# Gate and up weights of 32 experts: two strided transfers of 512 KB per tile, or one of 1 MB from weights laid out as tiles

## The chip, the cores and the metric

The kernel runs on one core of one Trainium2 chip. The metric is the device time of one execution in microseconds; the median of a few runs counts. One further execution was taken by the hardware profiler, and every row below comes from it.

## The reference, cut to what matters

One transformer block over 512 tokens of width 2048 in float32: a mixer (retention and a state space model), a mixture of 32 experts with two experts per token, a gated side input, and a last norm. The change touches only the weights of the experts:

```python
def expert_block(args):              # toks: the tokens of one block of expert e
    e, toks = args
    xb = ht[toks]
    a = jax.nn.silu(xb @ w_gate[e]) * (xb @ w_up[e])     # 2048 x 512 each
    return a @ w_down[e]                                 # 512 x 2048
```

Each expert has 4 MB of gate, 4 MB of up and 4 MB of down weights, 384 MB in all, and all of them are read.

## The kernel before

Three stages follow one another. The mixer takes the first 1300 us or so. Then comes the loop over the experts, in pairs (`pr`, two experts `ee` each), to about 2430 us. The last stage is the gated side input with its own weights.

**Tiles and their ring.** Every weight of an expert is loaded into SBUF as a tile of 128 partitions x 8 KB (1 MB). An expert takes 12 such tiles: 8 for gate and up (`load_gu`, q = 0 to 7) and 4 for down (`load_expert`). `mtile` hands out the tiles in turn from a ring of 13: six of pool `mwx` (on the right side of SBUF) and seven of pool `mw`. A transfer into a tile waits until TensorE has read what the tile held 13 tiles earlier. After expert 28 `mwx` is given up for other buffers (`right = False`), and experts 29 to 31 have a ring of seven.

**What a gate and up tile holds.** Partition p of tile q holds rows q*256 + p and q*256 + 128 + p of the gate and of the up matrix, in the order (k, w, f): k is the half of the 256 rows, w is gate or up, f the 512 columns. In HBM, gate and up are two tensors with rows of 512 floats, 2 KB. So a tile takes two transfers of 512 KB, one for gate and one for up, and each moves runs of 2 KB: two per partition. A down tile is 128 whole rows of 2048 floats: one transfer of 1 MB in runs of 8 KB.

**Order of the work.** All these transfers are issued by SyncE (SP), one after the other, in the order of the loop. TensorE (PE) also works in order. For one expert it runs 64 matmuls over the 8 gate and up tiles (line 991, into `pg`), waits for the activation on ACT and DVE (lines 994 to 996), transposes it (999), and runs 32 matmuls over the 4 down tiles (1008, into `py`). For a pair it also gathers the tokens (`dispatch_ids`, an indirect transfer of 1 MB issued by POOL into `xo`, line 854), transposes them (877), and adds the results into the residual (`combine`, 32 matmuls of line 1031 with additions on DVE, mixed with the next expert's gate and up matmuls). The matmul of one half k of a tile reads gate and up of that half together, so it needs both transfers of the tile.

**Beginning and end.** The first six tiles of expert 0 are loaded during the last product of the mixer; the others when that product's buffers are given up. The routing of the tokens to experts must be done before the first matmul of expert 0. In expert 29 `ple_side` loads the side input and its weights between q = 3 and q = 4, and its matmuls (1073) are mixed into the work of experts 29 to 31.

Behind the loop stands a second use of `load_expert`, for tokens beyond 64 of one expert; it is a loop over a count that is known only at run time.

Of the kernel before, what the change touches and what calls it, by code (L numbers as in the profile page):

```python
# [29 lines left out]
E, F = 32, 512  # L30
# [11 lines left out]
def kernel(ctx, tc, A, out):  # L42
    nc = tc.nc
# [93 lines left out]
    hT, wu = [], []  # L137
# [218 lines left out]
    for b in range(NB):  # L356
# [22 lines left out]
        for i, src in enumerate((c_re, c_im)):  # L379
            for g in range(2):  # L380
                q = slice(g * 64, (g + 1) * 64)
# [302 lines left out]
    ss2 = x1pool.tile([128, 4, 4], FT, name="ss2", bufs=1)  # L684
    lg = x1pool.tile([128, 512], FT, name="lg", bufs=1)

    wg_a, wu_a, wd_a = A["w_exp_gate"], A["w_exp_up"], A["w_exp_down"]
    NX, NM = 6, 7
    n_mw = 0
    right = True  # L690
# [1 line left out]
    def mtile():  # L692

        nonlocal n_mw
        n = n_mw % (NX + NM)
        n_mw += 1
        if right and n < NX:
            return mwx.tile([128, 2048], FT, name="mwx", tag="mwx", bufs=NX)
        return mw.tile([128, 2048], FT, name="mw", tag="mw", bufs=NM)

    def load_gu(wg, wu, q):
        t = mtile().rearrange("p (k w f) -> p k w f", k=2, w=2)
        for n, w in enumerate((wg, wu)):
            nc.sync.dma_start(t[:, :, n, :], w[q * 256:(q + 1) * 256, :].rearrange("(k p) f -> p k f", p=128))
        return t

    def load_expert(wg, wu, wd, between=None, have=()):
        gu, dn = list(have), []
        for q in range(len(gu), 8):
            if q == 4 and between is not None:  # L710
                between()
            gu.append(load_gu(wg, wu, q))
        for q in range(4):
            t = mtile()
            nc.sync.dma_start(t, wd[q * 128:(q + 1) * 128, :])
            dn.append(t)
        return gu, dn

    first = []
    for cb in range(4):  # L720
        sl = slice(cb * 512, (cb + 1) * 512)

        def ev_o(i, p, cb=cb, sl=sl):
            xn = x2[i][:, sl]
            V.tensor_tensor(xn, p, xn, op=OP.add)
            S.dma_start(x1_d[i * 128:(i + 1) * 128, sl], xn)
            jk = opool.tile([128, 512], FT, name="jk", tag="xt")
            S.activation(jk, xn, AF.Square, accum_out=ss2[:, i, cb:cb + 1])
        dense(A["w_out"], D, cb * 512, mT, "tok", ev_o)
        while len(first) < min(NX, 2 * (cb + 1)):  # L730
            first.append(load_gu(wg_a[0], wu_a[0], len(first)))
        pl = ps("pl")
        for d in range(4):
            pt = ps("pt")
            for i in range(4):
                PE.transpose(pt[:, i * 128:(i + 1) * 128], x2[i][:, cb * 512 + d * 128:cb * 512 + (d + 1) * 128], ident)
            xt = opool.tile([128, 512], FT, name="xt", tag="xt")
            (S.activation(xt, pt, AF.Copy) if d % 2 else V.tensor_copy(xt, pt))
            o = (d % 2) * 64
            PE.matmul(pl[o:o + 64, :], wr[:, cb * 4 + d, :], xt, start=d < 2, stop=d >= 2)  # L740
        if cb == 0:
            V.tensor_copy(lg, pl)
        else:
            V.tensor_tensor(lg, pl, lg, op=OP.add)
# [15 lines left out]

    io512 = mo.tile([128, T], FT, name="io512", bufs=1)
    with tc.high_priority(offset=8000):
        first = load_expert(wg_a[0], wu_a[0], wd_a[0], have=first)
    nc.sync.dma_start(io512, A["c_iota"])
    rtmp = tc.alloc_tile_pool(name="rtmp", bufs=1, reuse_waits="tile")

# [312 lines left out]
    for pr in range(E // 2):  # L1079
        _, xo, xg, tk1, _ = disp  # L1080
        nxt, sw_n = disp, sw
        ys = ytiles()
        for e in range(2):
            ee = pr * 2 + e
            if ee == E - 1:
                wg0 = gate_w(0, 0, 0, mtile().rearrange("p (k c) -> p k c", k=4))
            wts = load_expert(wg_a[ee], wu_a[ee], wd_a[ee], ple_side if ee == E - 3 else None) if ee else first
            if e == 0 and pr + 1 < E // 2:
                nxt = dispatch_ids(pr + 1)
                sw_n = dispatch_scales(nxt[0], pr + 1)  # L1090

            def xcol(kt):
                if ee == 0 and kt % 4 == 0:
                    dispatch_part(xo, xg, kt // 4)
                if kt % 2 == 0 and (ee != E - 3 or kt >= 8):
                    next(side, None)
                return xg[:, kt, e * CAP:(e + 1) * CAP]
            expert(wts, xcol, sw[:, e, 1:2], sw[:, e, 0:1], ys, e)
            if e == 0 and pr + 1 < E // 2:
                for d4 in range(4):  # L1100
                    dispatch_part(nxt[1], nxt[2], d4)
            if ee == E - 4:
                right = False
                mwx.release()
                x1pool.release()
                ple = tc.alloc_tile_pool(name="ple", bufs=1, side="right", reuse_waits="tile")
        disp = nxt
        sw = sw_n
        if pr == E // 2 - 1:
            for _ in side:  # L1110
                pass
        combine(ys, [tk1[:, v:v + 1] for v in range(2)])
# [5 lines left out]
    with tc.For_i(0, nov, 1) as bi:  # L1118
        ereg = nc.values_load(ctl_d[0:1, bass.ds(bi, 1)], engines=[mybir.EngineType.SP], min_val=0, max_val=E - 1,
                              skip_runtime_bounds_check_because="an expert's number, at most E - 1")  # L1120
        tbo = mo.tile([128, 4], FT, name="tbo", bufs=1)
        for hf in range(2):
            nc.sync.dma_start(tbo[hf * 64:hf * 64 + CAP], tbl_d[bass.ds(bi * CAP + E * CAP, CAP), :])
        oi = mo.tile([128, 1], I32, name="oi", bufs=2)
        V.tensor_scalar(oi, tbo[:, 0:1], 0.0, None, op0=OP.max)
        tko = mo.tile([128, 2], FT, name="tko", bufs=1)
        V.memset(tko, 0.0)
        for g in range(2):
            V.tensor_scalar(tko[g * 64:(g + 1) * 64, g:g + 1], tbo[g * 64:(g + 1) * 64, 0:1], 1.0, None, op0=OP.add)
        xo = xtile([128, D], "xo", "xo")  # L1130
        GP.indirect_dma_start(out=xo, out_offset=None, in_=x1_d,
                              in_offset=bass.IndirectOffsetOnAxis(ap=oi[:, 0:1], axis=0))
        xgo = xtile([128, 16, 128], "xgo")
        for d in range(16):
            px = ps("px")
            PE.transpose(px[:, :128], xo[:, d * 128:(d + 1) * 128], ident)
            V.tensor_scalar(xgo[:, d], px[:, :128], nffn[:, d:d + 1], None, op0=OP.mult)
        wts = load_expert(*(w[bass.ds(ereg, 1)].rearrange("o a b -> (o a) b") for w in (wg_a, wu_a, wd_a)))
        ys = ytiles()
        for y_ in ys:  # L1140
            V.memset(y_.bitcast(FT), 0.0)
        expert(wts, lambda kt: xgo[:, kt, 0:64], tbo[:, 1:2], tbo[:, 2:3], ys, 0)
        combine(ys, [tko[:, v:v + 1] for v in range(2)])
# [107 lines left out]
def host_arrays(inp):  # L1251

    g = {}
    f = np.ascontiguousarray
    g["x"] = f(inp["x"][0])
    g["xT"] = f(inp["x"][0].T)
    for k in ("norm_mix", "norm_ffn", "norm_ple"):
        g[k] = f(inp[k][0].reshape(16, 128).T)
    for k in ("w_in", "w_merge", "w_glu", "w_branch_a", "w_branch_b", "w_out",
              "w_exp_gate", "w_exp_up", "w_exp_down", "w_ple_gate", "w_ple"):  # L1260
        g[k] = f(inp[k][0])

    qk = g["w_in"][:, :2 * W].reshape(D, H, 2, 2, DH // 2).transpose(0, 1, 3, 2, 4).reshape(D, 2 * W)
    g["w_in"] = np.concatenate([qk, g["w_in"][:, 2 * W:]], axis=1)

    def gp(a):
        return a[0].reshape(NJ, 2, P, -1).transpose(1, 2, 0, 3).reshape(128, -1)

    ldt = np.broadcast_to(inp["ssm_log_dt"][0].reshape(NJ, 2).T[:, None, :], (2, P, NJ)).reshape(128, NJ)
    cr, ci = (inp[k][0].transpose(0, 2, 1)[None] for k in ("ssm_c_re", "ssm_c_im"))  # L1270
    dd = np.broadcast_to(inp["ssm_d"][0].reshape(NJ, 1, 2, C).transpose(1, 2, 3, 0), (L, 2, C, NJ)).reshape(128, NJ)
    g["s5_par"] = np.concatenate(
        [gp(inp["ssm_lam_re"][..., None]), gp(inp["ssm_lam_im"][..., None]), ldt, gp(inp["ssm_b_re"]),
         gp(inp["ssm_b_im"]), gp(cr), gp(ci), dd], axis=1)
    g["ret_gn_w"] = f(inp["ret_gn_w"][0].reshape(H, DH).T)
    g["norm_f"] = f(inp["norm_f"])
    g["pT"] = f(inp["p"][0, 0].T)
    g["w_router"] = f(np.concatenate([inp["w_router_group"][0], inp["w_router_expert"][0]], axis=1)
                      .reshape(16, 128, 36).transpose(1, 0, 2))
    g["b_router"] = np.concatenate([inp["b_router_group"][0], inp["b_router_expert"][0]])  # L1280
    return g
# [62 lines left out]
```

## Time and profile before

| what | us |
|---|---|
| median of 3 runs | 2632.17 (2630.09 to 2633.79) |
| the profiled execution, its own time | 2631.76 |
| its span, first to last instruction | 2630.0 |
| PE busy | 2470.2 (94%) |
| DVE busy | 1128.9 (43%) |
| ACT busy | 569.8 (22%) |
| mean granted TensorE clock | 0.987 of full |

The span is the stretch that the profile's rows cover; the profiled execution took 1.76 us more than its span. Ends of matmuls are modelled, and a matmul counts as busy also where it passes slowly, so PE at 94% is not PE at its peak. Two further things about the rows: times to landing of a transfer count from its issue, so they hold the time that it queues behind others; and the share of the DMA engines can come out somewhat over 1, since packets overlap.

### The profile page before, as it was taken

The numbers are of one execution on the slowest core, as the hardware profiler recorded it, in microseconds if no ns is written. First come the engines' busy times: TensorE is split into PE (matmuls) and PEld (weight loads), VectorE is DVE, ScalarE is ACT, GpSimd is POOL, SyncE is SP. The second block draws the span as 40 slices with busy tenths as digits, with TensorE's granted clock in tenths as the row PEclk, the third lists the DMA queues.
The fourth block names the chain that finished last, engine by engine and source line by source line (L and its number), as shares of the span: only waits on it lengthen the run. The fifth ranks groups of instructions, "written<-read, shape, count | busy, mean of one in ns | idle before, by whom it ended". The sixth has DMA issues, their size and how long they took to land. (4 is left out here: it accounts for less than half of the span.)

```text
span 2630.0 us, 28248 instructions
## 1 busy us (share of the span) xinstructions
PE 2470.2 (94%) x11178; PEld 1590.9 (60%) x11178; DVE 1128.9 (43%) x2204; ACT 569.8 (22%) x722; POOL 134.0 (5%) x166
## 2 busy tenths in 40 slices
PE   8999999999999999999969998888888888888998
PEld 7888788888888888887733333333333333323886
DVE  6648965333423443532244333333333333323535
ACT  4243222231221232222211000000000000012534
POOL 1010000002102010000010000000000000000101
PEclk9999999999999999999989999999999999999999
DMA  8332333442222245562279999999999999986333
GB/s 298 104 105 93 112 110 115 158 156 96 97 96 96 89 158 181 195 224 96 80 263 398 398 398 398 398 398 398 398 398 398 398 398 398 399 319 219 127 109 128
DMA packets 266023, 618.07 MB, mean 235 GB/s; under 512 B 19986, under 2 KB 28690, under 8 KB 246050
## 3 DMA queue, kind: packets, MB, share of 16 engines
q1 hardware_dynamic: 260208, 593.04, 61.9%
q0 software_dynamic: 3376, 19.01, 1.8%
q10 hardware_dynamic: 2306, 4.20, 0.4%
q8 instruction: 90, 1.47, 0.2%
q14 instruction: 43, 0.35, 0.0%
HBM read 591.01 MB, written 25.23 MB: 234 GB/s over the span
## 5 line engine op out<-in xcount | busy, mean ns | idle before, releaser
L63 DVE TENSOR_TENSOR wl<-wst,wh 128x2048 fp32r<-128x2048 f32 (+1 forms) x111 | 251.5, 2266 | 412.0 <-ACT wh L62 411.9
L103 PE MATMUL acc<-hTh,wh 128*128 128x512 f32 x832 | 327.9, 394 | 11.7 <-ACT wh L62 6.8
L62 ACT ACTIVATE wh<-wst 128x2048 fp32r<-128x2048 f32 (+1 forms) x111 | 207.5, 1869 | 605.6 <-PE acc L104 353.5
L104 PE MATMUL acc<-hTl,wh 128*128 128x512 f32 x832 | 328.5, 395 | 0.0
L105 PE MATMUL acc<-hTh,wl 128*128 128x512 f32 x832 | 326.0, 393 | 0.1
L991 PE MATMUL pg<-mw,xg 128*64 128x512 f32 x1136 | 289.6, 599 | 19.1 <-DMA mw<-in_w_exp_up_dram 19.1
L991 PE MATMUL pg<-mwx,xg 128*64 128x512 f32 x912 | 230.6, 600 | 10.0 <-DMA mwx<-in_w_exp_up_dram 9.4
L991 PEld LDWEIGHTS pg<-mw,xg 128*64 128x64 f32 x1136 | 81.2, 136 | 181.2 <-issue 177.4
L103 PEld LDWEIGHTS acc<-hTh,wh 128*128 128x128 f32 x832 | 157.4, 189 | 46.5 <-ACT wh L62 6.8
L1032 DVE TENSOR_TENSOR x<-pc,x 128x512 f32<-128x512 f32 x256 | 161.6, 684 | 40.8 <-PE pc L1031 40.4
L995 DVE SCALAR_TENSOR_TENSOR sg<-pg,sw,sg 128x256 f32<-128x256 f32 x32 | 15.5, 483 | 378.7 <-ACT sg L994 378.7
L104 PEld LDWEIGHTS acc<-hTl,wh 128*128 128x128 f32 x832 | 157.4, 189 | 33.2 <-issue 0.8
L105 PEld LDWEIGHTS acc<-hTh,wl 128*128 128x128 f32 x832 | 157.4, 189 | 33.2 <-DVE wl L63 0.8
L1016 DVE SCALAR_TENSOR_TENSOR ysl<-py,sw,ysh 64x512 fp32r<-64x512 f32 x128 | 94.8, 750 | 188.2 <-ACT ysh L1015 183.6
L1008 PE MATMUL py<-mw,aT 128*64 128x512 f32 x640 | 154.5, 622 | 4.1 <-DVE aT L1001 4.1
L1015 ACT ACTIVATE ysh<-py,sw 64x512 fp32r<-64x512 f32 x128 | 87.2, 682 | 293.8 <-PE py L1008 289.0
L991 PEld LDWEIGHTS pg<-mwx,xg 128*64 128x64 f32 x912 | 66.8, 137 | 136.3 <-issue 134.8
L994 ACT ACTIVATE sg<-pg,sw 128x256 f32<-128x256 f32 x32 | 15.2, 474 | 577.7 <-PE pg L991 577.7
L1031 PE MATMUL pc<-ysh,oht 128*128 128x512 f32 x256 | 107.5, 429 | 22.7 <-ACT ysh L1015 22.4
L1031 PEld LDWEIGHTS pc<-ysh,oht 128*128 128x128 f32 x256 | 48.5, 190 | 93.4 <-DVE x L1032 48.8
L1031 PE MATMUL pc<-ysl,oht 128*128 128x512 f32 x256 | 100.9, 404 | 0.0
L105 PE MATMUL acc<-wh,hTl 128*128 128x512 f32 x256 | 100.8, 394 | 0.0
(354 smaller groups left out, 3615.6 us busy)
## 6 DMA issues: line engine op xcount, KB each, us to landing
mw<-in_w_exp_down_dram SPq DMA_DIRECT2D x80, 1024.0 KB, 14.7
mw<-in_w_exp_gate_dram SPq DMA_DIRECT2D x142, 512.0 KB, 10.9
mw<-in_w_exp_up_dram SPq DMA_DIRECT2D x142, 512.0 KB, 10.8
mwx<-in_w_exp_gate_dram SPq DMA_DIRECT2D x114, 512.0 KB, 10.8
mwx<-in_w_exp_up_dram SPq DMA_DIRECT2D x114, 512.0 KB, 10.8
mwx<-in_w_exp_down_dram SPq DMA_DIRECT2D x48, 1024.0 KB, 15.8
wst<-in_w_in_dram SPq DMA_DIRECT2D x39, 1024.0 KB, 5.0
wst<-in_w_merge_dram SPq DMA_DIRECT2D x32, 1024.0 KB, 5.9
```

Of the source, the lines that this page charges most:

```text
L62: S.activation(hi, src, AF.Copy)
L63: V.tensor_sub(lo, src, hi.bitcast(FT))
L103: PE.matmul(acc, s0, m0, start=first, stop=False)
L104: PE.matmul(acc, s0, m1, start=False, stop=False)
L105: PE.matmul(acc, s1, m0, start=False, stop=last)
L991: PE.matmul(pg[hf * 64:(hf + 1) * 64, :], xk, gu[kt // 2][:, kt % 2, :, hf * 256:(hf + 1) * 256], start=kt == 0, stop=kt == 15)
L995: V.scalar_tensor_tensor(sg, pg[:, 0:256], rcol, sg, op0=OP.mult, op1=OP.mult)
L1008: PE.matmul(pys[c2][ch * 64:(ch + 1) * 64, :], aT[:, kc % 2, (kc // 2) * 64:(kc // 2 + 1) * 64], dn[kc][:, c0:c0 + 512], start=kc == 0, st ...
L1015: S.activation(yh[q, c0:c0 + 512], pys[c2][q], AF.Copy, scale=wcol[q])
L1016: V.scalar_tensor_tensor(yl[q, c0:c0 + 512], pys[c2][q], wcol[q], yh[q, c0:c0 + 512].bitcast(FT), op0=OP.mult, op1=OP.subtract)
L1031: PE.matmul(pc, oh[cb // 2][:, i * 128:(i + 1) * 128], ys[n][:, sl], start=n == 0, stop=n == 1)
L1032: V.tensor_tensor(x2[i][:, sl], pc, x2[i][:, sl], op=OP.add)
```

## The change

On the host, gate and up of each expert are written into one array in the order of the tiles: (expert, q, partition, k, w, f). Row q*128 + p of the new array is what partition p of tile q holds, 2048 floats, 8 KB in one piece. The kernel then loads a tile with one transfer of 1 MB. What lies where in SBUF is the same, and so is every matmul. The rest of the diff passes the one tensor where two were passed.

```diff
-    wg_a, wu_a, wd_a = A["w_exp_gate"], A["w_exp_up"], A["w_exp_down"]
+    wgu_a, wd_a = A["w_exp_gu"], A["w_exp_down"]
...
-    def load_gu(wg, wu, q):
-        t = mtile().rearrange("p (k w f) -> p k w f", k=2, w=2)
-        for n, w in enumerate((wg, wu)):
-            nc.sync.dma_start(t[:, :, n, :], w[q * 256:(q + 1) * 256, :].rearrange("(k p) f -> p k f", p=128))
-        return t
-
-    def load_expert(wg, wu, wd, between=None, have=()):
+    def load_gu(wgu, q):
+        t = mtile()
+        nc.sync.dma_start(t, wgu[q * 128:(q + 1) * 128, :])
+        return t.rearrange("p (k w f) -> p k w f", k=2, w=2)
+
+    def load_expert(wgu, wd, between=None, have=()):
...
-            gu.append(load_gu(wg, wu, q))
+            gu.append(load_gu(wgu, q))
...
-            wts = load_expert(wg_a[ee], wu_a[ee], wd_a[ee], ple_side if ee == E - 3 else None) if ee else first
+            wts = load_expert(wgu_a[ee], wd_a[ee], ple_side if ee == E - 3 else None) if ee else first
...
+    gu = np.empty((E, 8, 128, 2, 2, F), np.float32)
+    for n, k in enumerate(("w_exp_gate", "w_exp_up")):
+        gu[:, :, :, :, n] = inp[k][0].reshape(E, 8, 2, 128, F).transpose(0, 1, 3, 2, 4)
+    g["w_exp_gu"] = gu.reshape(E, 8 * 128, 4 * F)
```

## Rows read from the trace of the kernel before

**Rows 1.** The page: 40 slices of 65.75 us; DMA busy tenths, GB/s, packets.

```profile
DMA  8332333442222245562279999999999999986333
GB/s 298 104 105 93 112 110 115 158 156 96 97 96 96 89 158 181 195 224 96 80 263 398 398 398 398 398 398 398 398 398 398 398 398 398 399 319 219 127 109 128
DMA packets 266023, 618.07 MB, mean 235 GB/s; under 512 B 19986, under 2 KB 28690, under 8 KB 246050
```

**Rows 2.** The page, DMA issues: count, size, median us from issue to landing.

```profile
mw<-in_w_exp_down_dram SPq DMA_DIRECT2D x80, 1024.0 KB, 14.7
mw<-in_w_exp_gate_dram SPq DMA_DIRECT2D x142, 512.0 KB, 10.9
...
mwx<-in_w_exp_gate_dram SPq DMA_DIRECT2D x114, 512.0 KB, 10.8
```

**Rows 3.** Windows: length, busy of PE, PEld, DVE, ACT, POOL; clock, DMA share, GB/s.

```profile
1496.00:1512.00 16.00, 16.00 (x79) 5.76 (x81) 5.52 (x8) 2.73 (x4) 0.00 (x0) 1.00 1.05 386
1526.00:1542.00 16.00, 14.51 (x59) 6.77 (x55) 10.50 (x17) 2.73 (x4) 0.00 (x0) 1.00 1.05 387
1516.00:1522.00 6.00, 3.74 (x18) 1.05 (x16) 1.39 (x3) 0.47 (x1) 0.00 (x0) 1.00 1.01 421
1550.00:1558.00 8.00, 7.33 (x34) 2.16 (x30) 0.12 (x1) 0.47 (x1) 0.00 (x0) 1.00 1.02 423
...
1483.94:2274.88 790.94, 701.59 (x3122) 261.48 (x3120) 284.69 (x503) 76.90 (x120) 14.10 (x12) 0.98 1.04 398
```

**Rows 4.** Timeline of PE, one expert: start, us, line, [idle before <- releaser].

```profile
1699.43 7.04 PE L991 MATMUL pg<-mwx,xg 128*64 128x512 f32 x32
1707.12 1.94 PE L991 MATMUL pg<-mw,xg 128*64 128x512 f32 x8 [0.66 <-DMA mw<-in_w_exp_up_dram]
...
1715.23 1.94 PE L991 MATMUL pg<-mw,xg 128*64 128x512 f32 x8 [0.76 <-DMA mw<-in_w_exp_up_dram]
```

**Rows 5.** Timeline of POOL: the gathers of the tokens, one for each pair.

```profile
1483.94 1.18 POOL L854 DMA_INDIRECT xo<-x_d,oi  x1 [59.31 <-DVE oi L852]
...
1746.25 1.16 POOL L854 DMA_INDIRECT xo<-x_d,oi  x1 [66.36 <-DVE oi L852]
...
2274.88 1.17 POOL L854 DMA_INDIRECT xo<-x_d,oi  x1 [66.11 <-DVE oi L852]
```

**Rows 6.** Timeline of PE, from expert 0 to expert 2.

```profile
1374.59 0.41 PE L999 MATMUL pt<-ident,sg 128*128 128x128 f32 x2 [1.70 <-DVE sg L996]
...
1385.65 10.47 PE L991 MATMUL pg<-mwx,xg 128*64 128x512 f32 x48
...
1407.38 1.88 PE L991 MATMUL pg<-mw,xg 128*64 128x512 f32 x6
...
1433.28 0.44 PE L999 MATMUL pt<-ident,sg 128*128 128x128 f32 x2 [1.60 <-DVE sg L996]
```

**Rows 7.** Timeline of SP: issues at the beginning of the experts.

```profile
1335.91 0.47 SPq L704 DMA_DIRECT2D mw<-in_w_exp_up_dram  x1
1359.32 0.37 SPq L704 DMA_DIRECT2D mwx<-in_w_exp_gate_dram  x1
```

**Rows 8.** Waits of SP from 1484 to 2275: us, times, longest.

```profile
SPq L704 <- PE pg L991: 54.0, 22, 6.5
```

**Rows 9.** Timeline of PE: expert 29's last gate and up tile.

```profile
2315.78 1.94 PE L991 MATMUL pg<-mw,xg 128*64 128x512 f32 x8 [0.77 <-DMA mw<-in_w_exp_up_dram]
2319.41 0.41 PE L999 MATMUL pt<-ident,sg 128*128 128x128 f32 x2 [1.70 <-DVE sg L996]
```

**Rows 10.** Windows, as in rows 3: the first six tiles' loading, and experts 29 to 31.

```profile
1140.00:1180.00 40.00, 40.00 (x180) 33.13 (x179) 10.67 (x10) 8.37 (x10) 0.00 (x0) 1.00 0.81 280
2319.00:2430.00 111.00, 102.19 (x350) 35.55 (x350) 35.89 (x58) 19.72 (x32) 0.00 (x0) 0.98 0.69 251
```

**Rows 11.** DMA issues from 1483.94 to 2274.88: the gathers, median us to landing.

```profile
xo<-x_d,oi POOLq DMA_INDIRECT x12, 11.3
```

**Rows 12.** Timeline of PE: the first transposes of gathered tokens after 1746.

```profile
1757.78 0.77 PE L877 MATMUL px<-ident,xo 128*128 128x128 f32 x5
```

More of the change, by code (lines that the diff above doesn't have):

```diff
@@ L730 @@
         while len(first) < min(NX, 2 * (cb + 1)):
-            first.append(load_gu(wg_a[0], wu_a[0], len(first)))
+            first.append(load_gu(wgu_a[0], len(first)))
         pl = ps("pl")
@@ L762 @@
     with tc.high_priority(offset=8000):
-        first = load_expert(wg_a[0], wu_a[0], wd_a[0], have=first)
+        first = load_expert(wgu_a[0], wd_a[0], have=first)
     nc.sync.dma_start(io512, A["c_iota"])
@@ L1137 @@
             V.tensor_scalar(xgo[:, d], px[:, :128], nffn[:, d:d + 1], None, op0=OP.mult)
-        wts = load_expert(*(w[bass.ds(ereg, 1)].rearrange("o a b -> (o a) b") for w in (wg_a, wu_a, wd_a)))
+        wts = load_expert(*(w[bass.ds(ereg, 1)].rearrange("o a b -> (o a) b") for w in (wgu_a, wd_a)))
         ys = ytiles()
@@ L1259, in host_arrays @@
     for k in ("w_in", "w_merge", "w_glu", "w_branch_a", "w_branch_b", "w_out",
-              "w_exp_gate", "w_exp_up", "w_exp_down", "w_ple_gate", "w_ple"):
+              "w_exp_down", "w_ple_gate", "w_ple"):
         g[k] = f(inp[k][0])
+    gu = np.empty((E, 8, 128, 2, 2, F), np.float32)
+    for n, k in enumerate(("w_exp_gate", "w_exp_up")):
+        gu[:, :, :, :, n] = inp[k][0].reshape(E, 8, 2, 128, F).transpose(0, 1, 3, 2, 4)
+    g["w_exp_gu"] = gu.reshape(E, 8 * 128, 4 * F)
     qk = g["w_in"][:, :2 * W].reshape(D, H, 2, 2, DH // 2).transpose(0, 1, 3, 2, 4).reshape(D, 2 * W)
```

## The prediction

> **What bounds the kernel now.** I read the page's 40 slices first. The mixer and the last stage move 80 to 225 GB/s in most slices; in 14 slices, from about 1380 to 2300 us, the DMA engines are busy all the time and the rate stands at 398 GB/s without moving [rows 1]. A rate that doesn't move while the work on the other engines changes is the sign of a stage bound by transfers. The DMA issues say what is moved there: 256 gate tiles and as many up tiles of 512 KB (two names each, 142 and 114), and 128 down tiles of 1 MB [rows 2].
>
> Next I looked into the stage in short windows, to see whether 398 is one rate or a mean of two. It is a mean. While gate and up tiles pass, the engines move 386 or 387 GB/s; while down tiles (or the gather of the tokens) pass, 421 or 423, with the DMA share at 1.0 in both [rows 3]. The reader is to see that the two kinds differ in the length of their runs (2 KB and 8 KB), and that no engine's work goes along with it: in 1496 to 1512 PE is always busy and in 1526 to 1542 nearly so, at the same rate.
>
> Then I asked whether PE feels it. In the timeline of PE its matmuls over gate and up stand in groups of 8, one tile each, and at the end of an expert each group begins with a wait for a transfer: four groups begin from 1707.12 to 1715.23, 8.11/3 = 2.70 us apart [rows 4]. A tile of 1,048,576 bytes at 386.5 GB/s takes 2.713 us. So PE gets its tiles at the pace at which gate and up come in. Over many pairs: the gathers of the tokens begin 790.94/12 = 65.91 us apart [rows 5], and 12 is the number of pairs between the first and the last of them. In 65.91 us the queue moves 16 gate and up tiles, 8 down tiles and 1 MB of tokens. Taking 16 x 2.713 = 43.4 off, 22.5 us are left for 9 MB in 8 KB runs, 2.50 us each (419 GB/s). The windows and the pairs agree.
>
> **What PE would do without this wait.** At the beginning 13 tiles lie ready: the last of them is issued at 1335.91, and the next waits until 1359.32, when TensorE has freed one [rows 7]. So the first pairs show PE on its own. From the transpose in expert 0 (1374.59) to the same in expert 2 (1433.28) it takes 58.69 us, with 48 matmuls in 10.47 us in one piece and no transfer named before it [rows 6]. That is the other bound: a pair can't go under some 58.7 us, and 65.91 leaves 7.2 us of it as waiting.
>
> **The change part by part.**
>
> *The runs.* Each gate and up tile becomes what a down tile is now: 128 runs of 8 KB, 1 MB in one piece of HBM, one transfer, the same place in SBUF. The nearest row for its cost is thus the down tile itself. Bounds: 2.479 us (423 GB/s) and 2.506 us (22.55/9, the gather included). I take 2.50, since it comes from whole pairs and not from picked windows. A tile saves 2.713 - 2.50 = 0.213 us.
>
> *How many tiles count.* All that pass while the queue never runs dry. That begins with tile 13 (expert 1, q = 1) at 1359.32 and ends with expert 29, whose last tile PE still waits for at 2315.78 [rows 7, 9]. Expert 1 has 7 such tiles, experts 2 to 28 have 27 x 8 = 216, expert 29 has 8: 231. So 231 x 0.213 = 49.2 us. Expected pair: 16 x 2.50 + 9 x 2.50 = 62.5 us, 3.4 less than now and 3.8 above PE's 58.7; PE stays the one that waits.
>
> *Tiles that don't count.* The first six of expert 0 are loaded at 1140 to 1165 beside a PE that is busy 40 of 40 us [rows 10]; the next seven lie ready before the routing ends. Worth nothing, and if they were late they would cost no more than their own shortening. In experts 29 to 31 after 2319 the DMA share is 0.69 and PE is busy 102 of 111 us [rows 10]: PE sets the pace, and 16 faster tiles give 0 to 3.4 us. I take 0.
>
> *The issues.* 256 transfers fewer are issued by SP, 0.4 us each [rows 7]. SP is ahead of the transfers by the 10.8 us to landing [rows 2], so this is worth nothing now. If that cover were gone, 231 x 0.4 us would lie between transfers; fewer issues can only help then.
>
> *The waits.* A matmul needed gate and up of a tile, so it waited for the later of two; now it waits for one. Nothing becomes coarser. The ring stays at 13 tiles. SP waits for a free tile 54 us in 12 pairs, at most 6.5 us at once [rows 8], and the engines' share doesn't fall meanwhile [rows 3], since 10.8 us of transfers are queued. A faster queue runs ahead by some 38 us (the rest of a pair after a starved stretch, about 15 tiles) x 5% = 0.7 tile more, so the queue falls by about 2 us and still covers 6.5.
>
> **Rule against row.** In the first line of rows 3 the 2 KB runs move 386 GB/s, in the third the 8 KB runs 421: 9% apart. The Trainium skill, page DMA: Bandwidth & Descriptors, section Why small descriptors are slow, puts a fixed cost of about 3 cycles beside one per 32 B on each packet. An estimate from that page: 67 against 64.75 cycles per 2 KB, 3.4%, a tile of 2.62 us and 21 us in all. The measured rows give 49, and I hold to them.
>
> **The sum.** 0 for issues, waits, start and tail, -49.2 for the runs: span 2630.0 - 49.2 = 2580.8. The profiled execution took 2631.76, so 2582.6; the median of the runs lies 0.41 above it. I say 2583.
>
> **The rivals.**
>
> *8 KB runs don't hold 421 for long.* They come now only in bursts of some 4 or 5 tiles (10 to 13 us), so the rows don't show 900 us of them. If all runs together went at the mean that the stage has now, 398, a tile would take 2.635: 231 x 0.078 = 18 us, 2614. Against it: within a burst the rate doesn't sink. The estimate from the Trainium skill's page above would end near this, at 2611. Chance 0.07.
>
> *PE and the ring take over before 62.5.* PE's 58.7 was seen with full buffers. After a starved stretch PE's chain may be longer, and queue and PE can stall each other. If pairs settled at 64.0, about halfway between 62.5 and 65.9, 231/16 = 14.4 pairs would save 14.4 x 1.9 = 27 us: 2605. Against it: 3.8 us lie between the two bounds. Chance 0.12.
>
> *The change doesn't do what it says.* The rate could go with something else than the runs, as with the tensor read. Then the packets would fall by 256 x 384 = 98,304 and the time would stay: 2632. Against it: down and gathered tokens come from different tensors, by different queues, and both go at 421 or more. Chance 0.04.
>
> *Slower: the gather comes late.* It lands 11.3 us after its issue [rows 11]: issued at 1746.25, so at 1757.6, and PE reads it at 1757.78 [rows 5, 12], with the down matmuls behind it. It shares the 16 engines with SP's queue. If packets of 8 KB everywhere halve its part, it lands some 11 us later, PE's pair is 58.7 + 11 = 70, and 14 pairs cost 14 x 4 = 56 us; it decides from 7.2 us of delay on. With 9 us: 14 x 1.8 = 25, 2657. Against it: it passes mostly beside down tiles, 8 KB runs already [rows 3]. Chance 0.04.
>
> **How the numbers follow.** The forecast has 0.73. Its own range: 231 x (2.713 - 2.479) = 54 and 3.4 of the tail, 2574; 216 tiles x (2.70 - 2.506) = 42, 2590. For 8 in 10, I take in the second rival: 2573 to 2608. Under 0.2% (5.3 us) this kernel's measurement can't tell a change from none. Faster: 0.73 + 0.07 + 0.12 = 0.92; same 0.04; slower 0.04.
>
> **What would show it.** Right: 167,700 packets; the slices of the stage at 419 to 423 GB/s instead of 398; gathers 62.5 us apart; starved groups of PE 2.5 us apart; the last starved tile of expert 29 near 2267; from there to the end the same 310 us. The prediction is wrong if the slices show DMA shares under 1 (then the ring or PE stalls the queue), if pairs stay over 64, or if PE waits for `xo`.

## The result, and the profile after

| what | before | after |
|---|---|---|
| median, us | 2632.68 (4 runs) | 2591.05 (4 runs, 2589.92 to 2592.93) |
| ratio, 95% interval | | 0.9844 (0.9827 to 0.9861) |
| span of the profiled execution, us | 2630.0 | 2589.1 |

The kernel is 41.6 us faster. The forecast was 2583, with a range of 2573 to 2608: the direction and the range hold, and 8 of the 49 us are missing. Three lines of the page of the changed kernel (the slices are 64.73 us now):

```profile
DMA  8332333453323344663339999999999999885333
GB/s 303 106 103 86 116 120 110 144 167 98 106 90 98 106 128 163 215 217 129 98 152 416 413 421 413 419 421 416 420 421 417 421 421 417 362 323 222 119 102 130
DMA packets 163620, 618.02 MB, mean 239 GB/s; under 512 B 15890, under 2 KB 24594, under 8 KB 110882
```

The plateau stands at 413 to 421 GB/s instead of 398 [rows 1]. Packets fell by 98,304 as worked out, and by some 4,096 more under 512 B, 16 for each of the 256 transfers that are gone. But the plateau is no longer flat: slices of 419 to 421 alternate with 413 to 417. That is the first sign that something else holds the queue back now and then.

Windows of the changed kernel, in the same stretches as in [rows 3] and over 12 pairs:

```profile
1496.00:1512.00 16.00, 14.39 (x72) 5.51 (x70) 7.00 (x11) 3.20 (x5) 0.00 (x0) 1.00 1.01 421
1526.00:1542.00 16.00, 14.51 (x62) 6.05 (x57) 8.83 (x14) 2.73 (x4) 0.00 (x0) 1.00 1.02 422
1488.13:2238.89 750.76, 686.95 (x3122) 260.81 (x3120) 284.63 (x503) 76.89 (x120) 13.87 (x12) 0.99 1.01 419
```

Over whole pairs the rate is 419 GB/s, so gate and up pass at the rate of down now. Next, the gathers on POOL's timeline:

```profile
1488.13 1.18 POOL L853 DMA_INDIRECT xo<-x_d,oi  x1 [61.27 <-DVE oi L851]
1550.12 1.17 POOL L853 DMA_INDIRECT xo<-x_d,oi  x1 [60.81 <-DVE oi L851]
1613.83 1.17 POOL L853 DMA_INDIRECT xo<-x_d,oi  x1 [62.53 <-DVE oi L851]
...
2238.89 1.17 POOL L853 DMA_INDIRECT xo<-x_d,oi  x1 [60.81 <-DVE oi L851]
```

They lie 750.76 / 12 = 62.56 us apart, as forecast (62.5). Yet the reader is to see a pattern that a queue with a steady rate would not make: 62.0 and 63.7 us, two short to one long. And TensorE doesn't wait for weights any more: from 1484 to 2240 no wait of PE names a transfer. One pair on PE's timeline, with the end of expert 29:

```profile
2187.94 0.44 PE L998 MATMUL pt<-ident,sg 128*128 128x128 f32 x2 [1.60 <-DVE sg L995]
...
2199.33 10.47 PE L990 MATMUL pg<-mwx,xg 128*64 128x512 f32 x48
...
2222.72 0.49 PE L1030 MATMUL pc<-ysh,oht 128*128 128x512 f32 x1 [1.49 <-ACT ysh L1014]
...
2249.93 0.44 PE L998 MATMUL pt<-ident,sg 128*128 128x128 f32 x2 [1.60 <-DVE sg L995]
...
2278.99 0.41 PE L998 MATMUL pt<-ident,sg 128*128 128x128 f32 x2 [1.71 <-DVE sg L995]
```

From expert to expert it takes 61.99 us, and the waits in the brackets name DVE and ACT, no transfer. SP shows the other side of it, in its waits from 1484 to 2240:

```profile
SPq L703 <- PE pg L990: 301.1, 156, 9.4
```

SP waits 301 us for tiles that TensorE still reads, where it was 54 in a stretch of nearly the same length [rows 8]. The roles have changed.

### The profile page after: what moved, and what is told of

The parts are those of the page before. It is cut to its first block, busy times and chain, and to the rows that moved or that the text cites. A ratio compares the mean times of both kernels' runs of the same rounds, so it can differ in the third digit from the quotient of the medians.

```text
span 2589.1 us, 27740 instructions
## 1 busy us (share of the span) xinstructions
PE 2456.0 (95%) x11178; PEld 1588.2 (61%) x11178; DVE 1128.4 (44%) x2204; ACT 569.4 (22%) x722; POOL 133.7 (5%) x166
## 5 line engine op out<-in xcount | busy, mean ns | idle before, releaser
L990 PE MATMUL pg<-mw,xg 128*64 128x512 f32 x1136 | 284.3, 597 | 0.0
L1030 PE MATMUL pc<-ysh,oht 128*128 128x512 f32 x256 | 107.4, 428 | 22.7 <-ACT ysh L1014 22.4
L103 PE MATMUL accp<-wh,h3h 128*128 128x512 f32 x256 | 100.7, 394 | 0.0
```

The lines of the kernel that those rows point to most:

```text
L103: PE.matmul(acc, s0, m0, start=first, stop=False)
L990: PE.matmul(pg[hf * 64:(hf + 1) * 64, :], xk, gu[kt // 2][:, kt % 2, :, hf * 256:(hf + 1) * 256], start=kt == 0, stop=kt == 15)
L1030: PE.matmul(pc, oh[cb // 2][:, i * 128:(i + 1) * 128], ys[n][:, sl], start=n == 0, stop=n == 1)
```

## The experiments

The theory after this: the length of the runs made the rate, as forecast, and TensorE's own chain of 62 to 63.7 us a pair, not 58.7, stopped the gain. The rivals: it was the size or the number of transfers that made the rate; or the queue still bounds the kernel at 62.5. Unless it is said otherwise, the edits are made in the changed kernel, and ratios are to the kernel before. The diffs show the lines that matter; where a transfer needs its rows in another order, the host writes them so.

**Runs, transfers, sizes.** Four kernels keep the tiles in SBUF as they are and change only how they get there.

One transfer of 1 MB, runs of 2 KB:

```diff
-        nc.sync.dma_start(t, wgu[q * 128:(q + 1) * 128, :])
+        nc.sync.dma_start(t.rearrange("p (c f) -> p c f", c=4),
+                          wgu[q * 512:(q + 1) * 512, :].rearrange("(c p) f -> p c f", p=128))
```

> One transfer of 1 MB per tile, but the host leaves the rows apart, so that it moves runs of 2 KB, four per partition: the transfer size and count of the changed kernel with the runs of the one before. If the length of the runs makes the rate: 386 GB/s for gate and up, 398 in the mean, pairs 65.9 us apart, 2625 to 2635 us. If size or number makes it: 2588 to 2596 us.

Measured: 2631.52 us, ratio 1.000 (0.9989 to 1.0011). Its windows:

```profile
1496.00:1512.00 16.00, 14.40 (x72) 5.51 (x72) 7.02 (x11) 3.20 (x5) 0.00 (x0) 1.00 1.05 386
1526.00:1542.00 16.00, 14.51 (x56) 6.21 (x54) 8.23 (x13) 2.73 (x4) 0.00 (x0) 0.93 1.04 387
```

These are the rates of [rows 3] to the last digit. Half of the issues of gate and up are gone and nothing is gained: the number and size of the transfers were worth nothing. Nor was it worth anything to read one tensor in place of two, for this kernel reads one.

One transfer of 1 MB, runs of 4 KB:

```diff
-        nc.sync.dma_start(t, wgu[q * 128:(q + 1) * 128, :])
+        nc.sync.dma_start(t.rearrange("p (k c) -> p k c", k=2),
+                          wgu[q * 256:(q + 1) * 256, :].rearrange("(k p) c -> p k c", p=128))
```

> One transfer of 1 MB per tile with runs of 4 KB, two per partition. If every run costs a fixed extra time, the tile lies between 2.713 us (512 runs) and 2.49 (128 runs): with 256 runs 2.49 + 0.223 / 3 = 2.56 us, pairs at 16 x 2.56 + 22.4 = 63.4 us, queue still the bound over TensorE's 62.6, 2600 us or so. If only 2 KB is too short: as with 8 KB, 2591 us.

Measured: 2597.66 us, ratio 0.9869 (0.9841 to 0.9898). Its stage, a window over 12 pairs:

```profile
1487.01:2241.52 754.51, 689.39 (x3122) 261.02 (x3120) 284.46 (x503) 76.84 (x120) 13.87 (x12) 0.99 1.02 413
```

The 25 MB of tiles and tokens (26.2 million bytes) of a pair at 413 take 63.5 us, less 22.4 for down and gather 41.1, 2.57 us per tile: a fixed cost per run fits the three lengths. The pairs themselves were 62.9 us apart (754.51 / 12), since the ring still emptied: PE's first waits for weights come behind 2061 us, and until then its pairs take 62.0 or 63.7 us, as in the changed kernel.

Two transfers of 512 KB, runs of 4 KB (the edit is to the kernel above):

```diff
-        nc.sync.dma_start(t.rearrange("p (k c) -> p k c", k=2),
-                          wgu[q * 256:(q + 1) * 256, :].rearrange("(k p) c -> p k c", p=128))
+        for k in range(2):
+            nc.sync.dma_start(t[:, k * 1024:(k + 1) * 1024], wgu[q * 256 + k * 128:q * 256 + (k + 1) * 128, :])
```

> The weights laid out as for runs of 4 KB, but each tile loaded by two transfers of 512 KB, one for each half k, each over all 128 partitions in runs of 4 KB. Against the one transfer of 1 MB with the same runs (2597.7 us) only the number of transfers and their size differ. If the runs alone make the rate: 2595 to 2601 us, 413 GB/s. If 256 transfers more cost something of their own (0.1 us each would be 25 us): over 2610 us.

Measured: 2595.75 us, ratio 0.986 (0.9841 to 0.988); not to be told from the one transfer. The rate is the same too, in a long window of the stage:

```profile
1488.00:2230.00 742.00, 682.35 (x3046) 252.55 (x3042) 275.53 (x484) 76.92 (x120) 12.92 (x11) 0.98 1.02 413
```

One thing besides the transfers differs in the two kernels: PE's instructions came out in another order here, and without waits a pair takes 61.1 us. So the queue shows itself sooner: the last nine gaps between gathers are 63.4 us in the mean, near the 63.5 worked out for runs of 4 KB.

Two transfers of 512 KB, runs of 8 KB, 64 partitions each:

```diff
-        nc.sync.dma_start(t, wgu[q * 128:(q + 1) * 128, :])
+        for n in range(2):
+            ps_ = slice(n * 64, (n + 1) * 64)
+            nc.sync.dma_start(t[ps_], wgu[q * 128 + n * 64:q * 128 + (n + 1) * 64, :])
```

> Gate and up stay in tiles with 8 KB per partition, but each tile is loaded by two transfers of 512 KB, 64 partitions each: the runs of the changed kernel with the transfer size and count of the one before. If the length of the runs makes the rate: about 421 GB/s in the stage, pairs 62 to 63 us apart, 2588 to 2596 us. If the size or number of transfers makes it: 386 GB/s for gate and up, pairs near 65.9, 2625 to 2635 us.

Measured: 3320.89 us, ratio 1.2617 (1.2544 to 1.269). Neither theory had this. A long window of its stage:

```profile
1640.00:2900.00 1260.00, 824.95 (x2876) 270.32 (x2877) 265.14 (x466) 73.20 (x114) 12.93 (x11) 0.83 0.92 231
```

The DMA engines are 0.92 busy and move 231 GB/s: the packets themselves take longer. The gathers of eleven pairs, from 1664.56 to 2914.06, lie 113.6 us apart; less 22.5 us for down and gather, and divided by 16, that leaves some 5.7 us for a gate and up tile, 184 GB/s. So the experiment changed a third thing, the number of partitions that a transfer reaches, and the four-kilobyte pair above was made in its place. The Trainium skill, page SBUF — State Buffer, section Door 1: The DMA port swizzle, says that partitions 0 to 63 reach only 8 of the 16 ports of SBUF, and 64 to 127 the other 8, and gives 196 GB/s for a transfer of 64 partitions. Its section "Can I just issue two DMAs to hit both halves?" says that two such transfers at once gain only 6% over one. The 184 GB/s lie 6% under the first figure; that the ports are the cause is not shown by a run here.

**Who bounds the stage now.** Fewer bytes, the same work on the engines:

```diff
-    def load_expert(wgu, wd, between=None, have=()):
+    def load_expert(wgu, wd, between=None, have=(), half=False):
...
-            gu.append(load_gu(wgu, q))
+            gu.append(gu[-1] if half and q % 2 else load_gu(wgu, q))
...
-            wts = load_expert(wgu_a[ee], wd_a[ee], ple_side if ee == E - 3 else None) if ee else first
+            wts = load_expert(wgu_a[ee], wd_a[ee], ple_side if ee == E - 3 else None, half=e == 1 and ee < E - 4) if ee else first
```

> The changed kernel, but experts 1, 3, ... 27 load only every second gate and up tile and use each of these twice (so their products are made with other weights): 4 MB of 25 less per pair in 14 pairs, and every engine's work as before. If TensorE's own chain bounds the pairs of the changed kernel: pairs stay at 62.0 to 62.6 us, 2585 to 2592 us, with the DMA share near 0.85. If the queue bounds them: 10 us less per pair, some 2450 to 2480 us.

Measured: 2583.39 us, ratio 0.9815 (0.9786 to 0.9843). The stage moves 353 GB/s (a window from 1484 to 2240):

```profile
1484.00:2240.00 756.00, 695.06 (x3179) 264.95 (x3179) 285.96 (x509) 76.85 (x120) 15.04 (x13) 0.99 0.88 353
```

A sixth of the bytes is gone and 8 us of time, where a queue at its limit would have given 140. The 8 us, with which it comes out below both ranges, lie at the beginning: the pairs from the second on take 58.9, 58.7 and 60.4 us from gather to gather, and 62.4, 62.0 and 63.7 in the changed kernel, while the first takes 1.8 more. They go with an order of instructions, which the edit of the transfers changed without meaning to. In the timeline of PE, six matmuls of gate and up stand before the first one of the adding up in the second pair too, and in the third and fourth; in the changed kernel that is so in the first only.

```profile
1468.53 1.89 PE L1007 MATMUL py<-mwx,aT 128*64 128x512 f32 x8
1470.24 1.88 PE L990 MATMUL pg<-mwx,xg 128*64 128x512 f32 x6
1472.06 0.50 PE L1030 MATMUL pc<-ysh,oht 128*128 128x512 f32 x1
...
1496.11 0.43 PE L998 MATMUL pt<-ident,sg 128*128 128x128 f32 x2 [1.61 <-DVE sg L995]
...
1679.25 0.44 PE L998 MATMUL pt<-ident,sg 128*128 128x128 f32 x2 [1.60 <-DVE sg L995]
...
1741.24 0.44 PE L998 MATMUL pt<-ident,sg 128*128 128x128 f32 x2 [1.60 <-DVE sg L995]
```

From the end of the down products (1470.4) to the next transpose that takes 25.7 us; in the pair of the changed kernel shown above, where the adding up comes first and waits 1.49 us for ACT, it is 28.7 (from 2221.2). From the fifth pair on the order is that of the changed kernel, and so are the times: 61.99 us from 1679.25 to 1741.24, 62.0 or 63.7 in the pairs behind it, though the queue has a sixth less to move and no wait of PE names weights. So TensorE's chain holds these pairs, with its order in it.

Less work on TensorE and DVE, the same bytes, in the changed kernel and in the one before:

```diff
-            for cb in range(4):
+            for cb in range(0, 4, 4 // ncb):
...
-        combine(ys, [tk1[:, v:v + 1] for v in range(2)])
+        combine(ys, [tk1[:, v:v + 1] for v in range(2)], 2 if pr < 13 else 4)
```

> The changed kernel with half of the adding up of the pairs 0 to 12 left out (column blocks 1 and 3 of the four get nothing): some 3.7 us of TensorE's matmuls and 5.5 us of VectorE's additions less per pair, the transfers as they are. If TensorE's chain at 62.0 to 62.6 us lies just over the queue's 25 x 2.49 = 62.3: the pairs go to the queue's pace, the first ones shorter while the ring empties, the end of expert 29 comes some 8 to 10 us earlier, 2580 to 2584 us. If the queue bounds the changed kernel already: 2588 to 2592. If the queue can go faster than 62.3: pairs near 57 us, 2520 to 2540 us.

> The kernel before with the same half of the adding up left out. Its queue is the bound at 65.9 us a pair, so TensorE's shorter chain gives nothing: 2626 to 2633 us. If TensorE held part of the pairs, 2600 to 2620 us.

Measured: 2576.95 us (0.9793; 0.9773 to 0.9813) from the changed kernel, 2627.33 (0.9983; 0.9973 to 0.9994) from the one before. In the first, TensorE waits for weights again, in the rhythm of the queue (timeline of PE):

```profile
2118.92 1.94 PE L990 MATMUL pg<-mwx,xg 128*64 128x512 f32 x8 [0.55 <-DMA mwx<-in_w_exp_gu_dram]
2121.43 1.94 PE L990 MATMUL pg<-mwx,xg 128*64 128x512 f32 x8 [0.57 <-DMA mwx<-in_w_exp_gu_dram]
...
2131.37 1.94 PE L990 MATMUL pg<-mw,xg 128*64 128x512 f32 x8 [0.55 <-DMA mw<-in_w_exp_gu_dram]
...
2267.25 0.41 PE L998 MATMUL pt<-ident,sg 128*128 128x128 f32 x2 [1.71 <-DVE sg L995]
```

Six groups begin from 2118.92 to 2131.37, 2.49 us apart, and the transpose of expert 29 comes at 2267.25 instead of 2278.99. The same edit gave 14 us in the changed kernel (which came out 3 us under the range expected) and 4 to 5 in the one before. The profiled executions show where: in both some 5 us lie behind the transpose of expert 29, and what gave them was not traced. But between the first transpose and that one it is 895.4 us in place of 906.4 with the change, and 945.7 in place of 944.8 without it: 11 us against nothing. TensorE's work had become worth something.

**A version that uses it.** All of the work, but the adding up spread over the 16 steps of the next expert's gate and up (`steps` yields after each block, `ys` is taken from its pool only when the down products are done):

```diff
+                if kt:
+                    next(comb, None)
+                if kt == 15:
+                    next(comb, None)
                 return xg[:, kt, e * CAP:(e + 1) * CAP]
...
-        combine(ys, [tk1[:, v:v + 1] for v in range(2)])
+        comb = combine(ys, [tk1[:, v:v + 1] for v in range(2)])
```

> The changed kernel with all of its work, in another order: the adding up of a pair is not written in one piece but one block of 512 columns after each of the 16 steps of gate and up of the next expert, so that VectorE's additions (0.68 us each) lie under TensorE's 0.86 us of gate and up. If TensorE's chain is the bound, it falls to some 57 or 58 us, the queue's 62.3 takes over: 2574 to 2584 us. If the queue is the bound already: 2588 to 2592 us, less 3 us at most in experts 30 and 31.

> The same order of the adding up in the kernel before, with its two transfers of 2 KB runs. The queue bounds it, so only the last two pairs can gain: 2624 to 2633 us. If TensorE's chain held it too: under 2620 us.

Measured: 2579.15 us, ratio 0.98 (0.9784 to 0.9816), and 2630.26 (0.9996; 0.9985 to 1.0006) in the kernel before. The same edit is worth 12 us behind the change and nothing measurable ahead of it. Over 12 pairs the window of the first is

```profile
1463.95:2200.64 736.69, 676.95 (x3122) 253.58 (x3120) 282.49 (x500) 76.83 (x120) 11.26 (x13) 0.98 1.01 421
```

so 61.4 us a pair, with the queue at 421 GB/s in the mean. TensorE's chain did not fall to 57 or 58 us, as was expected, but to 60.4, and 62.1 in pairs where the down products run slowly; its trace has, for the most part, three blocks behind every eight products, not one behind each step. Waits for weights come only behind 2140 us, in the last pairs. From the first transpose to that of expert 29 it takes 895.1 us, as long as the experiment with less work (895.4). Two more kernels asked what holds this version. The first adds the edit of fewer bytes to it; the second is to move three blocks to where TensorE waits for the activation:

```diff
-                if kt:
-                    next(comb, None)
-                if kt == 15:
-                    next(comb, None)
+                if kt > 2:
+                    next(comb, None)
...
+        for _ in range(3):
+            next(comb, None)
         pt = ps("pt")
```

> The kernel with the adding up spread over the next expert's products (2579 us), and experts 1, 3, ... 27 load only every second gate and up tile and use each twice, so their products are made with other weights: 4 MB of 25 less per pair. If the queue's 62.3 us holds that version: 2550 to 2570 us. If TensorE's chain holds it too (its gathers are 60.4 or 62.1 us apart): 2573 to 2580 us.

> The kernel with the adding up spread, of whose 16 blocks three now come where TensorE waits for the activation after gate and up (1.6 to 2.7 us idle), 13 between gate and up: TensorE's chain 1.4 us shorter per pair. If TensorE still holds that version: 2565 to 2575 us for 14 pairs x 1.4 at most, as far as the queue lets it, with a floor of some 2573. If the queue holds it: 2576 to 2580, as without.

Measured: 2577.5 us (0.9791; 0.9771 to 0.9811) with fewer bytes, 2576.25 (0.9784; 0.9768 to 0.9801) with three blocks meant for the gap. Neither can be told from 2579.15. With fewer bytes the pairs still take 60.4 or some 62 us from the fifth on, and the stretch between the two transposes falls only from 895.1 to 890.9 us: over all of it TensorE's chain lies some 4 us under the queue. The second did not do what was meant. Its PE timeline has no block in the gap, and the transpose waits as long as in the version without the edit (1.61 us):

```profile
1984.35 0.50 PE L1036 MATMUL pc<-ysl,oht 128*128 128x512 f32 x1
1984.78 1.94 PE L992 MATMUL pg<-mw,xg 128*64 128x512 f32 x8
1986.55 1.89 PE L992 MATMUL pg<-mwx,xg 128*64 128x512 f32 x8
1990.05 0.44 PE L1002 MATMUL pt<-ident,sg 128*128 128x128 f32 x2 [1.62 <-DVE sg L997]
```

So its time says nothing on the queue. That less work of TensorE alone would not help this version either is suggested by the two equal stretches (895.1 and 895.4 us), and not shown by an edit to it. As far as the runs go, the two bounds have met within some 4 us of 895.

## Why the prediction was right, and where it was off

*What bounds the kernel before: right.* The queue did: half of the adding up taken away, or spread, moved it by 0.2% or less.

*The runs: right, in mechanism and size.* 386 became 421, and with runs of 2 and of 4 KB neither the number nor the size of the transfers has a part in it. With TensorE out of the way the term is nearly exact: from the first transpose (1371.9) to that of expert 29 (2267.25) the experiment with less TensorE work takes 895.4 us. The forecast is 944.8 (1374.59 [rows 6] to 2319.41 [rows 9]) less 49.2, 895.6; the spread version comes to 895.1.

*Tiles that don't count, issues, waits: right as far as seen.* From the transpose of expert 29 to the end it is 310.1 us, 310.6 before. The first transpose came 2.0 us earlier (1372.58). The forecast had nothing for that, and nothing says that the change gave it: over all kernels here but that with 64 partitions it comes between 1371.8 and 1374.7, and two with the old transfers stand at the two ends.

*What TensorE would do without the wait: wrong, and this is the step that cost the 8 us.* The forecast took 58.69 us from the first pair [rows 6], because its tiles lay ready, and had PE stay the one that waits. But the instructions of each pair are written out singly, in an order of their own, and the first pair has the good one: six matmuls of gate and up before the adding up. The later pairs don't. The trace of before had shown it in the next two pairs. Two lines of PE's timeline of the kernel before, with no transfer named between them or from 1433.28 [rows 6] to the first:

```profile
1494.97 0.44 PE L999 MATMUL pt<-ident,sg 128*128 128x128 f32 x2 [1.60 <-DVE sg L996]
...
1558.93 0.44 PE L999 MATMUL pt<-ident,sg 128*128 128x128 f32 x2 [1.60 <-DVE sg L996]
```

That is 61.69 and 63.96 us of TensorE's own. With 62.0, or 62.56 with the slow thirds, its bound lies as high as the queue's (62.5, or 62.3 at 2.49 us a tile), and TensorE's is the one that holds. From the first transpose to expert 29's the changed kernel takes 906.4 us: 14.5 pairs of 62.5. The queue could have done it in 895.4, as the experiment with less TensorE work shows. Some 4 of the 11.0 us that TensorE keeps come from the first pair alone (a late gather and a lower clock, below), the rest from its pace in the others. The 2.0 at the start and 0.5 at the end hide a part of them; that is luck.

*The spacing of 62.5 was right by luck.* It was forecast as the queue's and came out as TensorE's, which happens to be as long. The list of what would show the forecast right asked for this number; only the waits told the two apart: no group of PE starved, against the 2.5 us that it had named.

*The rivals.* TensorE taking over was the second, at 0.12; it happened, but at 62.56 and not at 64, and by the order of its instructions and its slow thirds, not by a stall of the ring. That the rate goes with the tensor read is refuted: from one tensor, runs of 2 KB pass at 386. Of the late gather the changed kernel shows one case, in its first pair (timeline of PE):

```profile
1374.37 1.30 PE L876 MATMUL px<-ident,xo 128*128 128x128 f32 x5 [1.38 <-DMA xo<-x_d,oi]
1375.60 9.26 PE L1007 MATMUL py<-mw,aT 128*64 128x512 f32 x32
```

The wait is 1.38 us. More went to the clock, which was granted at 0.50 from 1374 to 1380: the 32 down matmuls took 9.26 us, where they took 7.09 in the same place of the kernel before. That pair took 62.9 us instead of 58.7. Whether the wait brought the lower clock on is not shown.

That runs of 8 KB don't hold 421 for long is refuted by the windows above. The estimate from the Trainium skill, page DMA: Bandwidth & Descriptors, section Why small descriptors are slow (3.4% between the two lengths), is too low here: 386 against 421 is 9%.

## What to carry to other kernels

A queue that is always busy can be bound by more than bytes: compare its rate between stretches with different run lengths, and if they differ, lay the data out for the longer runs; merging transfers without that gave nothing here. Before a wait is counted as gain, take the other engine's own pace from a typical repetition and not from the first one, since in an unrolled program each repetition can have an order of its own. An edit to the transfers can change that order too, and an edit to the order can come to nothing, so look at the timeline before a time is put down to an edit. When two bounds come out within 1% of each other, work on both: the order of the adding up was worth nothing before the change and 12 us behind it.

## What the runs showed of the hardware that was not expected

The 64-partition transfers: two of 512 KB in place of one of 1 MB, with the same runs, took a tile from 2.49 to some 5.7 us, while the DMA engines counted as 0.92 busy. Busy DMA engines were no sign of a good rate.

The cost of a run is a steady one: a tile took 2.71 us with 512 runs of 2 KB, 2.57 with 256 of 4 KB and 2.49 with 128 of 8 KB, some 0.58 ns more for each run (0.223 us over 384, from the first and the last), which is 9 ns of one of 16 engines.

The granted clock goes with the slow third of the pairs. Windows of the changed kernel:

```profile
1588.00:1590.00 2.00, 2.00 (x8) 0.49 (x5) 0.00 (x0) 0.00 (x0) 0.00 (x0) 0.56 0.98 410
1590.00:1592.00 2.00, 2.00 (x8) 0.63 (x6) 0.00 (x0) 0.00 (x0) 0.00 (x0) 0.59 1.03 430
```

For most of these 4 us the clock is at the lower of its two levels, 1.2 of 2.4 GHz, just after TensorE had been idle for the activation (1.71 and 0.52 us). The 32 down matmuls there span 8.79 us; in the pair shown first they span 7.09, behind the same idle times. So these alone don't decide on which pair it falls, and what does stays open.
